# A token axis of 544 columns in halves of 272, where it had 546 in parts of 256 and 290

## The chip, the core and the metric

The kernel runs on one core of a Trainium2 chip. Its engines are named as the profile names them: PE is TensorE's matrix unit and PEld its weight loads, DVE is VectorE, ACT is ScalarE, POOL is GpSimd and SP is SyncE. The metric is the device time of one execution in microseconds (us), and a kernel's time is the median of its runs. The TensorE clock that was granted over the profiled execution of the kernel before is 0.999 of full speed, which is the upper one of its two levels, 2.4 GHz.

## The reference

One inference step of a two-layer encoder for two request groups: a prompt of 512 tokens and a sample of 32 tokens with caches. Everything is fp32. Cut to what the change touches:

```python
def conv_ffn(h, hist, w_up, conv_w, conv_b, w_down):
    S = h.shape[1]
    g, up = jnp.split(h @ w_up, 2, axis=-1)
    gp = jnp.concatenate([hist, g], axis=1)
    c = conv_b + sum(conv_w[j] * gp[:, j:j + S] for j in range(CONV_W))
    a = jax.nn.silu(c) * up
    return a @ w_down, gp[:, -(CONV_W - 1):]

def trunk_layer(x, pos, past_k, past_v, mem_k, mem_v, conv_hist, w, lam_init):
    h = rmsnorm(x, w['norm_mix_g'])
    z = h @ w['w_in']
    ...
    x = x + jnp.concatenate([o, g_out], axis=-1) @ w['w_out']
    x = x + cross_attend(rmsnorm(x, w['norm_x_g']), mem_k, mem_v, ...)
    f, conv_state = conv_ffn(rmsnorm(x, w['norm_ffn_g']), conv_hist, ...)
    return x + f, k, v, gv, conv_state
```

The model has 1024 features and 2816 hidden features of the FFN (22 tiles of 128). The convolution runs over three tokens: a token's own gate row and the two before it. The prompt starts with two rows of zeros, the sample with the two rows of `state_ffn_conv`.

## The kernel before

**The token axis.** Most of the network is computed with features on the 128 partitions and tokens along the free axis. Prompt and sample lie side by side on one axis of T = 546 columns: 512 prompt tokens, 2 columns of padding (set to zero in most tiles), and 32 sample tokens from column S0 = 514. The two padding columns serve the convolution: the tile of gate rows `gb` has two zero columns, then the 546 token columns, and the sample's two history rows are copied into the padding, so that one shifted pass over the whole tile computes the convolution of both groups.

**Exact products.** A weight tile is loaded raw by DMA (SP's queue), then split by ACT (L133) and DVE (L134) into a high and a low part, `hl[:, 0]` and `hl[:, 1]`; activations are split likewise. `hx` (the residual, [128, 8, 2, T]), `at` (the FFN's hidden rows, [128, 2, T]), `og` and `gg` (mixer outputs) and `co` (cross-attention outputs) hold the high part in `[.., 0, :]` and the low part in `[.., 1, :]`, in fp32r, 4 bytes an element. So the low part of a row starts T x 4 = 2184 bytes behind the high part.

**The projections.** `proj_fm` (its matmul is L263) makes one output tile of 128 features for all tokens. For each k tile it makes three passes: weights high x activations high, weights high x activations low, weights low x activations high. Each pass is a pair of matmuls, one for each part of the token axis in NSPL, into two PSUM banks whose tiles end in "a" (256 columns) and "b" (290 columns). The stationary operand is a 128 x 128 block of weights and the moving operand is a part of an activation row:

```python
for hl, ks, first, last in parts:
    for j, (kk, rh, rl) in enumerate(ks):
        for wpart, mv, st in ((0, rh, True), (0, rl, False), (1, rh, False)):
            for n0, nn in NSPL:
                pe.matmul(out=ps[0 if n0 == 0 else 1][:, 0:nn], ...
                          rhs=mv[:, n0:n0 + nn], ...)
```

A projection of 8 k tiles is 24 pairs (`pfg` and `pfu` of the FFN's gate and up rows, `pq`, `pu`, `pwo`, `pwc`); a down projection of the FFN (`pfd`) has 11 k tiles in each half of the hidden features, 33 pairs. Other projections (`tm_group`, L280 to L282, tiles `pr` and `pm`) have tokens on partitions: their stationary operand is an activation block, and their moving operand is the weight tile itself, 256 columns, first `hl[:, 0]`, then `hl[:, 1]`, then `hl[:, 0]`. The cross-attention's output (L875, `pxo`) moves the whole 512 columns of a tile `pT` of the prompt alone.

**The FFN.** For a hidden tile f: the gate projection into `pfga` and `pfgb`; DVE scales both into `gb` (L910); POOL clears two columns (L908), copies the sample's history into `gb` (L911) and keeps the last rows in `fc` (L912, L913); ACT makes the convolution's first term (L914); DVE adds the other two (L917); ACT and DVE finish SiLU (L919, L920); and the up projection, multiplied in, is split into `at`. PSUM has three pairs of banks for these projections.

**The order of the work.** Each engine runs its own queue in order. A tile framework schedules the instructions of each engine by a simulated timeline of its own, so that the order in a queue isn't quite that of the source, and it adds the semaphore waits. Pools with a fixed number of buffers (5 of the tag that `gb`, `ct`, `th` and `up` share) make a writer wait until a buffer's last reader is done.

Of the kernel before, what the change touches and what calls it, by code (L numbers as in the profile page):

```python
# [13 lines left out]
ALU = mybir.AluOpType  # L14
# [4 lines left out]
SP = 512  # L19
# [6 lines left out]
T = 546          # tokens on the free axis: 512 prompt, 2 of padding, 32 sample  # L26
S0 = 514         # first sample token
NSPL = ((0, 256), (256, 290))
# [5 lines left out]
def encoder_step(ctx: ExitStack, tc: tile.TileContext, a, o):  # L34
# [31 lines left out]
    f32 = lambda ap: ap.bitcast(F32)  # L66
    MP = (slice(0, 64), slice(64, 128))

# [85 lines left out]
    def rsq(v, p, n, name, eng=vec):  # L154
        """1/sqrt of a compact tile: bit-level first guess, three Newton steps."""
        y, h, t = (tp.tile([128, n], F32, tag=f"{name}_{v}", bufs=2 if v == "y" else 1, name=name + v)
                   for v in "yht")
        yy, hh, tt = y[0:p, 0:n], h[0:p, 0:n], t[0:p, 0:n]
        eng.tensor_scalar(out=yy.bitcast(I32), in0=v.bitcast(I32), scalar1=-0.5, scalar2=1597463007.0,
                          op0=ALU.mult, op1=ALU.add)  # L160
        eng.tensor_scalar(out=hh, in0=v, scalar1=-0.5, scalar2=None, op0=ALU.mult)
        for _ in range(3):
            eng.tensor_tensor(out=tt, in0=yy, in1=yy, op=ALU.mult)
            eng.tensor_tensor(out=tt, in0=tt, in1=hh, op=ALU.mult)
            if eng is vec:
                vec.scalar_tensor_tensor(out=yy, in0=tt, scalar=1.5, in1=yy, op0=ALU.add, op1=ALU.mult)
            else:
                eng.tensor_scalar(out=tt, in0=tt, scalar1=1.5, scalar2=None, op0=ALU.add)
                eng.tensor_tensor(out=yy, in0=tt, in1=yy, op=ALU.mult)
        return y  # L170
# [5 lines left out]
    def gelu2(z, t):  # L176
        """z <- 2 * gelu(z), tanh form"""
        act.activation(out=t, in_=z, func=AF.Square, scale=math.sqrt(0.044715))
        vec.scalar_tensor_tensor(out=t, in0=t, scalar=1.0, in1=z, op0=ALU.add, op1=ALU.mult)
        act.activation(out=t, in_=t, func=AF.Tanh, scale=GC)  # L180
        vec.scalar_tensor_tensor(out=z, in0=t, scalar=1.0, in1=z, op0=ALU.add, op1=ALU.mult)

# [1 line left out]
    ssq_t = {}  # L184

    def set_hx(kt, g):
        """the gained residual as hi + lo"""
        xv = x[:, kt]
        act.activation(out=hx[:, kt, 0], in_=xv, func=AF.Copy, scale=g[:, kt:kt + 1])
        vec.scalar_tensor_tensor(out=hx[:, kt, 1], in0=xv, scalar=g[:, kt:kt + 1], in1=f32(hx[:, kt, 0]),  # L190
                                 op0=ALU.mult, op1=ALU.subtract)

    def set_sq(kt):
        """the sum of the residual's squares"""
        sq = tmp([128, T], "sqx")
        act.activation(out=sq, in_=x[:, kt], func=AF.Square)
        if kt == 0:
            ssq_t["x"] = G("t4", [128, T], "ssq")
            pool.tensor_copy(ssq_t["x"], sq)
        else:  # L200
            pool.tensor_tensor(out=ssq_t["x"], in0=ssq_t["x"], in1=sq, op=ALU.add)
# [16 lines left out]
    def x_stats(need_bc):  # L218
        """per token: v = mean square + eps, eps * v and 1/sqrt(v)"""
# [25 lines left out]
        pool.memset(rbc[:, SP:S0], 0.0)  # L245
        for i in range(2):
            pb = psS("pbc")
            for t in range(2):
                pe.matmul(out=pb[:, 128 * t:128 * t + 128], lhsT=ones, rhs=dg[:, 2 * i + t], start=True, stop=True)
            if i == 1:  # L250
                pe.matmul(out=pb[:, 256:288], lhsT=ones[0:32], rhs=dgs, start=True, stop=True)
                act.copy(rbc[:, S0:T], pb[:, 256:288])
            act.copy(rbc[:, 256 * i:256 * i + 256], pb[:, 0:256])  # L253
        return r, ve, rbc

# [1 line left out]
    def proj_fm(ps, col, parts):  # L257
        """features on partitions; parts: (weights [128, 2, n, 256], [(k in unit, rhs hi, rhs lo)], first, last)"""
# [111 lines left out]
    def load_consts2(l):  # L370
        """wider per-layer constants"""
# [11 lines left out]
    def norm_rope(z, p, nt, ss, rs, c, t0):  # L383
        """z [p, nt, 256] in place: QK-norm with 1/rms rs [p, nt * 4], gains, rotary"""
# [43 lines left out]
    def kq_T(l, h, z, zs):  # L428
        # of map m the rows MP[m] carry k's hi part, the others its lo part; q's hi part stands on both
# [45 lines left out]
    def softmax_diff(ps, p, n, e, c, name):  # L475
        """e[:, 0] <- exp(S0 - max) - lam * (sum0 / sum1) * exp(S1 - max); returns the sums"""
# [14 lines left out]
    def take_o(po, p, ot, ss):  # L491
        """head output rows out of PSUM, and their squares' sum"""
        junk = tmp([128, 128], "junk", tag="oh", bufs=1)
        act.copy(ot, po)
        act.activation(out=junk[0:p], in_=po, func=AF.Square, accum_out=ss)

    def subnorm(ot, sso, s0, p, n, name):
        """ot [p, n, 128]: head outputs; sso: their squares' sums; s0: softmax sums, where not yet divided by"""
# [77 lines left out]
    def do_attn_sample_end(l, hp, og, st):  # L576
        """the sample's head outputs of a pair of heads: norm, transpose"""
# [59 lines left out]
    def do_gate(l, j, vn, zs, ws):  # L637
        """the spatial gates of a pair of groups"""
        c = LC[l]
        res = []  # L640
        for jj in range(2):
# [10 lines left out]
            pool.memset(s[:, SP:S0], 0.0)  # L652
# [11 lines left out]
    def do_u(j, w2, rbc):  # L664
        """u of one group, times 2"""
        ps = psR2("pu")
        proj_fm(ps, j, x_parts(w2))
        u = tmp([128, T], "u")
        t1 = tmp([128, T], "ut")
        for v, n0, nn in halves(ps):  # L670
            vec.tensor_tensor(out=u[:, n0:n0 + nn], in0=v, in1=rbc[:, n0:n0 + nn], op=ALU.mult)
        gelu2(u, t1)
        return u
# [51 lines left out]
    def do_mem_k(l, h, mt, vm):  # L725
# [25 lines left out]
        # cached memory keys of the sample  # L751
# [23 lines left out]
    def do_cross_q(l, h, ve):  # L775
# [4 lines left out]
        for dc in range(2):  # L780
# [8 lines left out]
            act.copy(qs[:, dc], ps[1][:, S0 - 256:T - 256])  # L789
# [21 lines left out]
    def do_cross_scores(h, mk, cmT, qq):  # L811
# [36 lines left out]
        # sample tokens  # L848
# [42 lines left out]
    def do_ffn(l, rbc, after):  # L891
# [3 lines left out]
        for hf in range(2):  # L895
            av = []
            for f0 in range(hf * HF, hf * HF + HF, 2):
# [3 lines left out]
                for f in fs:  # L901
# [9 lines left out]
                    pool.tensor_copy(gb[:, SP + 2:SP + 4], c["st"][:, :, f])  # L911
# [4 lines left out]
                    for jj in (1, 0):  # L916
                        vec.scalar_tensor_tensor(out=ct, in0=gb[:, jj:jj + T], scalar=c["cw"][:, jj, f:f + 1],  # L917
                                                 in1=ct, op0=ALU.mult, op1=ALU.add)
                    act.activation(out=th, in_=ct, func=AF.Tanh, scale=0.5)  # L919
# [60 lines left out]
    for kt in range(8):  # L980
# [4 lines left out]
        vec.memset(ps[1][:, 256:258], 0.0)  # L985
        pe.transpose(ps[1][:, 258:290], xs[:, 128 * kt:128 * kt + 128], ident[0:32, 0:32])
        for i, (v, n0, nn) in enumerate(halves(ps)):
            (vec.tensor_copy if i else act.copy)(x[:, kt, n0:n0 + nn], v)
# [9 lines left out]
    for l in range(DEPTH):  # L998
# [5 lines left out]
        for t in og:  # L1004
            pool.memset(f32(t[:, :, SP:S0]), 0.0)
# [46 lines left out]
        for h in range(4):  # L1052
# [7 lines left out]
            for dc in range(2):  # L1060
                t = G(COTAGS[2 * h + dc], [128, 2, T], "co", F32R)
                pool.memset(f32(t[:, :, SP:S0]), 0.0)
# [27 lines left out]
def _rope_table():  # L1090
    """cos and signed sin of the rotary angles by position: a constant of the shapes alone"""
# [31 lines left out]
```

## Time and profile before

| | |
|---|---|
| time, median of 3 runs | 1721.8 us (1720.87 to 1721.93) |
| the profiled execution's own span | 1721.5 us |
| PE busy | 1700.7 us, 99% of the span, 13115 matmuls |
| PEld busy | 1641.7 us, 95% |
| DVE busy | 996.2 us, 58% |
| ACT busy | 728.9 us, 42% |
| POOL busy | 220.3 us, 13% |
| DMA | 158.03 MB, mean 92 GB/s |

The page gives one execution; the span runs from the first to the last instruction and is the only time of its own that the execution has, 0.3 us under the median. A matmul's duration in the profile overlaps that of the next one, since matmuls are pipelined; the time from one start to the next is what a matmul takes of the span. Both are read below.

### The profile page before, as it was taken

To read this page: it belongs to the slowest core of one execution; us is meant where nothing else is said; L and a number is where in the kernel's file an instruction comes from. 1 tells how busy PE (TensorE), PEld (TensorE's weight loads), DVE (VectorE), ACT (ScalarE), POOL (GpSimd) and SP (SyncE) were. 2 spreads that over 40 slices of the span, in tenths; PEclk is the share of its full clock that TensorE was granted. 3 is DMA by queue.
4 is the path that set the end of the run, shared out by engine and by line. 5 is a ranking of instruction groups with operands and counts; after the bars stand their busy time and mean duration, and the time that the engine had idled before them with its cause. 6 is when DMAs were issued, how large, how long until landed. Compare 5 with 4: busy or idle time off the path is not lost.

```text
span 1721.5 us, 32408 instructions
## 1 busy us (share of the span) xinstructions
PE 1700.7 (99%) x13115; PEld 1641.7 (95%) x13115; DVE 996.2 (58%) x2138; ACT 728.9 (42%) x1485; POOL 220.3 (13%) x624
## 2 busy tenths in 40 slices
PE   7999999999999999999999999999999999999998
PEld 6988899999999999999998888999999999999998
DVE  6778765565466624655367677655555665255642
ACT  5456754455333312333345576445543332133321
POOL 4000014221200000000111000422221000000000
PEclk9999999999999999999999999999999999999999
DMA  5222233442222233223332222243422322333131
GB/s 174 89 86 71 66 102 100 141 130 82 86 79 88 70 88 108 86 68 87 93 117 70 76 69 85 85 130 105 129 81 74 99 62 86 101 94 90 55 115 57
DMA packets 200988, 158.03 MB, mean 92 GB/s; under 512 B 8670, under 2 KB 200038, under 8 KB 200838
## 3 DMA queue, kind: packets, MB, share of 16 engines
q1 hardware_dynamic: 200774, 155.82, 29.8%
q8 instruction: 103, 1.69, 0.4%
q14 instruction: 47, 0.39, 0.1%
q10 hardware_dynamic: 64, 0.14, 0.0%
HBM read 144.83 MB, written 11.10 MB: 91 GB/s over the span
## 4 chain that ended last, share of the span: by engine, by line
PE 95%; ACT 1%; POOL 1%; DVE 1%; issue 1%; SPq 1%; DMA 0%; ACTq 0%; DVEq 0%
PE pfgb L263 8%; PE pfub L263 8%; PE pfdb L263 8%; PE pfua L263 7%; PE pfga L263 7%; PE pfda L263 7%; PE pr L282 4%; PE pr L280 4%; PE pr L281 4%; PE pwob L263 3%; PE pqb L263 3%; PE pwcb L263 3%; PE pwoa L263 3%; PE pwca L263 3%; PE pqa L263 3%; PE pub L263 2%
## 5 line engine op out<-in xcount | busy, mean ns | idle before, releaser
L134 DVE TENSOR_TENSOR hl<-raw,hl 128x1024 fp32r<-128x1024 f32 (+2 forms) x280 | 317.1, 1133 | 278.0 <-ACT hl L133 277.6
L133 ACT CAST hl<-raw 128x1024 fp32r<-128x1024 f32 (+2 forms) x280 | 269.9, 964 | 408.8 <-PE pfdb L263 139.2
L263 PE MATMUL pfgb<-hx,hl 128*128 128x290 f32 x1056 | 269.6, 297 | 0.0
L263 PE MATMUL pfdb<-at,hl 128*128 128x290 f32 x1056 | 269.5, 298 | 0.0
L263 PE MATMUL pfga<-hx,hl 128*128 128x256 f32 x1056 | 269.3, 283 | 0.0
L263 PE MATMUL pfda<-at,hl 128*128 128x256 f32 x1056 | 268.4, 282 | 0.0
L263 PE MATMUL pfub<-hx,hl 128*128 128x290 f32 x1056 | 264.9, 297 | 0.0
L263 PE MATMUL pfua<-hx,hl 128*128 128x256 f32 x1056 | 264.2, 283 | 0.5 <-ACT rbc L253 0.5
L263 PEld LDWEIGHTS pfdb<-at,hl 128*128 128x128 f32 x1056 | 200.4, 190 | 0.1
L263 PEld LDWEIGHTS pfgb<-hx,hl 128*128 128x128 f32 x1056 | 200.4, 190 | 0.0
L263 PEld LDWEIGHTS pfda<-at,hl 128*128 128x128 f32 x1056 | 200.0, 189 | 0.0
L263 PEld LDWEIGHTS pfga<-hx,hl 128*128 128x128 f32 x1056 | 199.6, 189 | 0.0
L263 PEld LDWEIGHTS pfub<-hx,hl 128*128 128x128 f32 x1056 | 198.3, 190 | 0.0
L263 PEld LDWEIGHTS pfua<-hx,hl 128*128 128x128 f32 x1056 | 196.9, 189 | 0.7 <-ACT rbc L253 0.7
L282 PE MATMUL pr<-hl,hx 128*128 128x256 f32 x512 | 147.8, 290 | 2.4 <-DVE hx L190 2.4
L280 PE MATMUL pr<-hl,hx 128*128 128x256 f32 x512 | 147.5, 289 | 1.4 <-DVE vs L305 0.9
L281 PE MATMUL pr<-hl,hx 128*128 128x256 f32 x512 | 147.6, 289 | 0.8 <-DVE hl L134 0.8
L282 PEld LDWEIGHTS pr<-hl,hx 128*128 128x128 f32 x512 | 98.0, 192 | 5.8 <-DVE hx L190 2.8
L281 PEld LDWEIGHTS pr<-hl,hx 128*128 128x128 f32 x512 | 98.3, 192 | 3.6 <-issue 1.7
L280 PEld LDWEIGHTS pr<-hl,hx 128*128 128x128 f32 x512 | 98.0, 192 | 3.7 <-DVE vs L305 1.1
L263 PE MATMUL pwcb<-co,hl 128*128 128x290 f32 x384 | 88.7, 298 | 0.0
L917 DVE SCALAR_TENSOR_TENSOR ct<-gb,cols,ct 128x546 f32<-128x546 f32 x88 | 69.3, 787 | 33.2 <-ACT ct L914 31.6
(360 smaller groups left out, 3312.7 us busy)
## 6 DMA issues: line engine op xcount, KB each, us to landing
raw<-in_w_up_dram SPq DMA_DIRECT2D x80, 512.0 KB
raw<-in_w_down_dram SPq DMA_DIRECT2D x32, 512.0 KB
raw<-in_w_in_dram SPq DMA_DIRECT2D x24, 512.0 KB
raw<-in_w_in_dram SPq DMA_DIRECT2D x32, 256.0 KB
raw<-in_w_out_dram SPq DMA_DIRECT2D x32, 256.0 KB
raw<-in_wq_c_dram SPq DMA_DIRECT2D x16, 512.0 KB
raw<-in_wk_c_dram SPq DMA_DIRECT2D x16, 512.0 KB
raw<-in_wv_c_dram SPq DMA_DIRECT2D x16, 512.0 KB
```

The costliest lines, as they stand in the source:

```text
L133: act.copy(hl[:, 0, 0:n * wc], raw[:, 0:n * wc])
L134: vec.tensor_tensor(out=hl[:, 1, 0:n * wc], in0=raw[:, 0:n * wc], in1=f32(hl[:, 0, 0:n * wc]), op=ALU.subtract)
L263: pe.matmul(out=ps[0 if n0 == 0 else 1][:, 0:nn], lhsT=hl[:, wpart, kk, col * 128:col * 128 + 128], rhs=mv[:, n0:n0 + nn], start=first and ...
L280: pe.matmul(out=out, lhsT=lh(k), rhs=hl[:, 0, k % 4], start=(k == 0), stop=False)
L281: pe.matmul(out=out, lhsT=lh(k), rhs=hl[:, 1, k % 4], start=False, stop=False)
L282: pe.matmul(out=out, lhsT=ll(k), rhs=hl[:, 0, k % 4], start=False, stop=(k == k8 - 1))
L917: vec.scalar_tensor_tensor(out=ct, in0=gb[:, jj:jj + T], scalar=c["cw"][:, jj, f:f + 1], in1=ct, op0=ALU.mult, op1=ALU.add)
```

## The change

The two padding columns go: T is 544, the sample starts at column 512, and the two parts of the axis are equal halves of 272. The memsets of the padding go with it (in `rbc`, `s`, `og`, `co` and the input's PSUM tile), and the two copies of `rbc`'s second part become one. The convolution can no longer find the sample's history in `gb`. It runs over all 544 columns as before, which leaves the first two sample columns of `ct` wrong, and these two are computed apart: `gs` is a tile of four columns (two of history, two of the sample's first gate rows), `ge` one of two columns; three more POOL instructions and two more DVE instructions for each of the 44 hidden tiles (22 in each layer) take the place of one POOL copy.

```diff
-T = 546          # tokens on the free axis: 512 prompt, 2 of padding, 32 sample
-S0 = 514         # first sample token
-NSPL = ((0, 256), (256, 290))
+T = 544
+S0 = 512
+TH = T // 2
+NSPL = ((0, TH), (TH, TH))
...
-        pool.memset(rbc[:, SP:S0], 0.0)
...
-                act.copy(rbc[:, S0:T], pb[:, 256:288])
-            act.copy(rbc[:, 256 * i:256 * i + 256], pb[:, 0:256])
+            act.copy(rbc[:, 256 * i:256 * i + 256 + 32 * i], pb[:, 0:256 + 32 * i])
...
-            pool.memset(s[:, SP:S0], 0.0)
...
-            act.copy(qs[:, dc], ps[1][:, S0 - 256:T - 256])
+            act.copy(qs[:, dc], ps[1][:, S0 - TH:T - TH])
...
-                    pool.tensor_copy(gb[:, SP + 2:SP + 4], c["st"][:, :, f])
+                    gs = tiny([128, 4], "gs")
+                    ge = tiny([128, 2], "ge")
+                    pool.tensor_copy(gs[:, 0:2], c["st"][:, :, f])
+                    pool.tensor_copy(gs[:, 2:4], gb[:, S0 + 2:S0 + 4])
+                    pool.tensor_scalar(out=ge, in0=gs[:, 2:4], scalar1=c["cw"][:, 2, f:f + 1],
+                                       scalar2=c["cb"][:, f:f + 1], op0=ALU.mult, op1=ALU.add)
                     pool.tensor_copy(fc[:, 0:2, f], gb[:, SP:SP + 2])
                     pool.tensor_copy(fc[:, 2:4, f], gb[:, T:T + 2])
                     act.activation(out=ct, in_=gb[:, 2:T + 2], func=AF.Identity, scale=c["cw"][:, 2, f:f + 1],
...
                     for jj in (1, 0):
                         vec.scalar_tensor_tensor(out=ct, in0=gb[:, jj:jj + T], scalar=c["cw"][:, jj, f:f + 1],
                                                  in1=ct, op0=ALU.mult, op1=ALU.add)
+                    vec.scalar_tensor_tensor(out=ge, in0=gs[:, 1:3], scalar=c["cw"][:, 1, f:f + 1], in1=ge,
+                                             op0=ALU.mult, op1=ALU.add)
+                    vec.scalar_tensor_tensor(out=ct[:, S0:S0 + 2], in0=gs[:, 0:2], scalar=c["cw"][:, 0, f:f + 1],
+                                             in1=ge, op0=ALU.mult, op1=ALU.add)
...
-        vec.memset(ps[1][:, 256:258], 0.0)
-        pe.transpose(ps[1][:, 258:290], xs[:, 128 * kt:128 * kt + 128], ident[0:32, 0:32])
-        for i, (v, n0, nn) in enumerate(halves(ps)):
-            (vec.tensor_copy if i else act.copy)(x[:, kt, n0:n0 + nn], v)
+        pe.transpose(ps[1][:, 256:288], xs[:, 128 * kt:128 * kt + 128], ident[0:32, 0:32])
+        act.copy(x[:, kt, 0:256], ps[0][:, 0:256])
+        vec.tensor_copy(x[:, kt, 256:T], ps[1][:, 0:288])
...
-        for t in og:
-            pool.memset(f32(t[:, :, SP:S0]), 0.0)
...
-                pool.memset(f32(t[:, :, SP:S0]), 0.0)
```

The change makes each activation row 544 x 4 = 2176 bytes long, which is 34 x 64; 546 x 4 = 2184 bytes was 34 x 64 + 8. The second half starts at byte 1088 = 17 x 64 of its row, where it started at byte 1024 = 16 x 64. The tiles that L263 moves start at multiples of 32 bytes, `hx` at a multiple of 64, before and after; so with 2176 every part starts at a multiple of 32, and with 2184 every low part of a row starts 8 bytes off a multiple of 16.

DVE's queue in the FFN, from a gate projection's scaling to the end of SiLU (first layer; `hl` rows belong to the weight stream). Before:

```order
L910 TENSOR_TENSOR gb<-pfga,rbc 128x256
L910 TENSOR_TENSOR gb<-pfgb,rbc 128x290
L917 SCALAR_TENSOR_TENSOR ct<-gb,cols_253,ct 128x546 x2
L134 TENSOR_TENSOR hl<-raw,hl 128x512
L920 SCALAR_TENSOR_TENSOR ct<-th,ct 128x546
```

The same place now (`cols` holds the convolution's weights):

```order
L908 TENSOR_TENSOR gb<-pfga,rbc 128x272
L908 TENSOR_TENSOR gb<-pfgb,rbc 128x272
L923 SCALAR_TENSOR_TENSOR ge<-gs,cols_245,ge 128x2
L921 SCALAR_TENSOR_TENSOR ct<-gb,cols_245,ct 128x544 x2
L925 SCALAR_TENSOR_TENSOR ct<-gs,cols_245,ge 128x2
L135 TENSOR_TENSOR hl<-raw,hl 128x512
L928 SCALAR_TENSOR_TENSOR ct<-th,ct 128x544
```

The scheduler has put the first small step, which reads `ge` from POOL, right behind the scaling and ahead of the two long steps, which wait for ACT.

POOL's queue between two gate projections of the same stretch (`st` is the sample's history). Before:

```order
L908 MEMSET gb 128x2
L911 COPY gb<-st_259 128x2
L912 COPY fc<-gb 128x2
L913 COPY fc<-gb 128x2
L908 MEMSET gb 128x2
```

The same place now:

```order
L906 MEMSET gb 128x2
L913 COPY gs<-gb 128x2
L916 COPY fc<-gb 128x2
L917 COPY fc<-gb 128x2
L914 TENSOR_SCALAR ge<-gs,cols_245 128x2
L912 COPY gs<-st_251 128x2
L906 MEMSET gb 128x2
```

The history's copy no longer stands between the scaling and ACT's first term: it goes into `gs`, ahead of the next projection. The step that DVE waits for, L914, stands fourth behind the scaling.

## Rows read from the trace of the kernel before

**Rows 1.** Busy time of engines, from the page.

```profile
PE 1700.7 (99%) x13115; PEld 1641.7 (95%) x13115; DVE 996.2 (58%) x2138; ACT 728.9 (42%) x1485; POOL 220.3 (13%) x624
```

**Rows 2.** PE's waits: for what, total us, times, longest.

```profile
PE pxina L983 <- DMA xin<-in_x_prompt_dram: 5.3, 1, 5.3
...
PE pfua L263 <- ACT rbc L253: 0.5, 2, 0.2
```

**Rows 3.** L263 by group: count | busy us, mean ns | idle before.

```profile
L263 PE MATMUL pfgb<-hx,hl 128*128 128x290 f32 x1056 | 269.6, 297 | 0.0
...
L263 PE MATMUL pwcb<-co,hl 128*128 128x290 f32 x384 | 88.7, 298 | 0.0
...
L263 PE MATMUL pub<-hx,hl 128*128 128x290 f32 x192 | 39.3, 307 | 0.0
```

**Rows 4.** 100 us of FFN: busy us and count of PE, PEld, DVE, ACT, POOL; clock.

```profile
700.00:800.00 100.00, 100.00 (x788) 100.00 (x788) 61.89 (x93) 34.43 (x44) 4.72 (x31) 1.00 0.26 78
```

**Rows 5.** PE's timeline in down projections: start us, duration us, line, tiles.

```profile
600.29 0.30 PE L263 MATMUL pfub<-hx,hl 128*128 128x290 f32 x1
600.43 0.29 PE L263 MATMUL pfda<-at,hl 128*128 128x256 f32 x1
...
608.80 0.28 PE L263 MATMUL pfda<-at,hl 128*128 128x256 f32 x1
...
609.04 0.29 PE L263 MATMUL pfda<-at,hl 128*128 128x256 f32 x1
...
609.30 0.28 PE L263 MATMUL pfda<-at,hl 128*128 128x256 f32 x1
...
609.55 0.28 PE L263 MATMUL pfda<-at,hl 128*128 128x256 f32 x1
...
609.81 0.29 PE L263 MATMUL pfda<-at,hl 128*128 128x256 f32 x1
...
610.07 0.28 PE L263 MATMUL pfda<-at,hl 128*128 128x256 f32 x1
...
610.32 0.28 PE L263 MATMUL pfda<-at,hl 128*128 128x256 f32 x1
...
610.57 0.28 PE L263 MATMUL pfda<-at,hl 128*128 128x256 f32 x1
...
610.83 0.28 PE L263 MATMUL pfda<-at,hl 128*128 128x256 f32 x1
...
611.08 0.28 PE L263 MATMUL pfda<-at,hl 128*128 128x256 f32 x1
```

**Rows 6.** PE's timeline in a stream of 256-column matmuls with weights moving.

```profile
292.58 0.28 PE L281 MATMUL pm<-hl,memT 128*128 128x256 f32 x1
292.69 0.28 PE L282 MATMUL pm<-hl,memT 128*128 128x256 f32 x1
...
303.81 0.29 PE L282 MATMUL pm<-hl,memT 128*128 128x256 f32 x1
```

**Rows 7.** PE's timeline around six matmuls of 512 columns.

```profile
358.94 1.57 PE L875 MATMUL pxo<-pT,mvs 128*128 128x512 f32 x6
360.35 0.84 PE L263 MATMUL pqb<-hx,hl 128*128 128x290 f32 x5
```

**Rows 8.** Timeline of DVE, POOL and ACT behind one gate projection.

```profile
704.30 0.45 DVE L910 TENSOR_TENSOR gb<-pfgb,rbc 128x290 f32<-128x290 f32 x1
704.81 0.19 POOL L911 COPY gb<-st 128x2 f32<-128x2 f32 x1 [5.64 <-DVE gb L910]
...
705.05 0.84 ACT L914 ACTIVATE ct<-gb,cols 128x546 f32<-128x546 f32 x1
705.18 1.23 DVE L134 TENSOR_TENSOR hl<-raw,hl 128x1024 fp32r<-128x1024 f32 x1 [0.43 <-ACT hl L133]
706.32 0.78 DVE L917 SCALAR_TENSOR_TENSOR ct<-gb,cols,ct 128x546 f32<-128x546 f32 x1
```

**Rows 9.** Small instructions by group: count | busy us, mean ns | idle before.

```profile
L733 DVE SCALAR_TENSOR_TENSOR mss<-mss,vm 128x2 f32<-128x2 f32 x8 | 1.2, 148 | 0.0
L168 POOL TENSOR_SCALAR rmkt<-rmkt 128x2 f32<-128x2 f32 x24 | 5.4, 223 | 2.1
L985 DVE MEMSET pxinb<- 128x2 f32 x8 | 0.5, 60 | 2.0 <-PE pxinb L983 2.0
L1062 POOL MEMSET co<- 128x4 f32 x16 | 1.6, 103 | 51.8 <-PE pg L646 30.2 <-PE pmt L709 17.7 <-PE pwob L263 3.9
```

## The prediction

> **What bounds the kernel now.** I begin with the page's busy times. PE is busy for 1700.7 of 1721.5 us, so it stands still for 20.8 us; DVE works for 58% and POOL for 13% [rows 1]. Since overlapped matmuls can look busy without being at their peak, I then ask for PE's waits. The longest is the first load of the input, 5.3 us; of the terms that the change touches, PE waits 0.5 us in all for the copies of `rbc` [rows 2]. So no stall is worth removing here, and the time is the number of matmuls times what each takes from start to start.
>
> Most of them are those of `proj_fm`. Its second-half matmuls count 1056 each in `pfg`, `pfu` and `pfd` (the row of one stands), 384 each in `pwc` and `pq`, 192 each in `pu` and the two kinds of `pwo`, with no idle time before them worth a term [rows 3]: 3 x 1056 + 2 x 384 + 3 x 192 = 4512 pairs. The durations there (297 to 307 ns) are not the price, for they overlap. The price is in the stretch from 700 to 800 us, which is FFN alone: 788 matmuls in 100 us at a granted clock of 1.00 [rows 4], 126.9 ns each, 253.8 ns a pair of 256 and 290 columns. All pairs together are 4512 x 253.8 ns = 1145 us, two thirds of the span.
>
> **What the change does to a pair.** It takes 2 of 546 columns away, evens out the halves, and moves the start of every second row. I price these from streams.
>
> First the columns. The tokens-on-partitions products move weights in blocks of 256 columns, from tiles whose parts all start at multiples of 32 bytes: 95 starts after 292.58 us the stream is at 303.81 [rows 6], 118.2 ns each. Six matmuls of 512 columns, also from such a tile, take from 358.94 to 360.35 [rows 7], 235 ns each. Between the two lengths a column costs (235 - 118.2) / 256 = 0.456 ns. Two columns less are 0.91 ns a pair, 4512 x 0.91 = 4.1 us in all.
>
> Then the halves. On that line 256 and 290 columns would take 118.2 + 133.7 = 251.9 ns, and twice 272 takes 2 x (118.2 + 16 x 0.456) = 251.0. A straight line doesn't care how 544 is shared out, so evening out by itself is worth nothing. But the pairs take 253.8 and not 251.9: something costs 1.9 ns more than the line.
>
> What that is, the down projections show. They begin at 600.43, where `pfd` follows `pfu`; one is 33 pairs, so the next begins 33 x 0.2538 = 8.37 us later, at 608.80 [rows 5]. From there the starts of the first half follow the code's three passes (high, low, low weights). Over three k tiles the first passes take 0.24, 0.26, 0.25, the second 0.26, 0.26, 0.26, the third 0.25, 0.25, 0.25 us: 0.250 a pair where the high part of `at` is moved, 0.260 where the low part is. The low part is what starts 2184 bytes further on, 8 bytes off every multiple of 16. That the values are low, or that the second pass has the weights of the first, isn't it by the other stream: there L281 moves the low part of a tile as well, against the stationary block of L280, and the low part starts 4096 bytes behind the high one; its step to the next start is 0.11 us, no longer than the mean of 0.118 [rows 6]. So I put the extra time down to where the row starts. From what multiple on a start is a good one, these rows can't say; 2176 keeps all of those that the high parts have.
>
> With the change the low parts start as the high ones do. For a pair afterwards I have two values. By the line it is 251.0. By the high passes in the down projections it is 250.0 less two columns, 249.1. The second comes from one tile group with starts read to 10 ns; the first rests on long streams, though of other operands. I take 250.6, nearer to the line. The saving is 3.2 ns a pair, 4512 x 3.2 = **14.4 us**. The ends are 253.8 - 249.1 = 4.7 ns, or 21.2 us, and the two columns alone, 4.1 us.
>
> The Trainium skill, "TensorE: Matmul & The Clock Gate", section "Back-to-back issue gap", gives an isolated warm matmul N / 2.4 + 2.5 ns, with no term for an operand's address. An estimate from it is 232.5 ns for a pair before and 231.7 after, 3.8 us in all over these pairs; the trace disagrees with its level (253.8) and agrees roughly with its slope (0.456 against 0.417 ns a column). By that rule only the columns would count, which is the first rival below.
>
> **What it does elsewhere.** Eight DVE memsets of 60 ns go from the input, and POOL memsets of about 0.1 us each from `co`, `og`, `s` and `rbc` [rows 9]. PE waits for none of them for more than the 0.5 us of `rbc` [rows 2], so I count nothing; the uncovered price of all is some 4 us of POOL time (36 memsets of 103 ns) and 0.5 of DVE's.
>
> The convolution loses one POOL copy (0.19 us [rows 8]) and gains three POOL instructions and two on DVE for each of 44 hidden tiles. The nearest rows for these are 0.15 us for a 128 x 2 step on DVE and 0.22 for one on POOL [rows 9]; so DVE has 0.3 us more to do in each, 13 us in all, and POOL about 0.4. Where they lie matters more. DVE's first small step now stands right behind the scaling and waits for POOL's fourth instruction. The scaling ended at 704.75, POOL's copy started at 704.81 and ACT's first term at 705.05 [rows 8]; four POOL steps of about 0.2 us put `ge` at some 705.6. What is queued behind that step is the weight split of DVE, which in this place started at 705.18, and the long steps, which ran from 706.32. The split could thus start 0.4 us later. ACT's first term no longer waits for POOL's copy and may start 0.2 us sooner. Who waits for all that is PE, through PSUM banks and weights; but a gate projection takes 24 x 0.254 = 6.1 us, there are three pairs of banks, and DVE works for 62% of this stretch [rows 4]. I take 0. If that cover were gone, 44 x (0.3 + 0.4) = 31 us would be the price.
>
> The sum: 1721.5 - 14.4 = 1707.1 us for the execution profiled, whose span is 0.3 under the median of the runs; so 1707.4 us as a median.
>
> **The rivals.** A change of 0.2% (3.4 us) is about what a measurement of this kernel can tell from none.
>
> *Only the columns count.* Then the slow second pass has another cause and stays: 253.8 - 0.91 = 252.9 a pair, 1721.8 - 4.1 = 1717.7 us. For it speaks that the rows show starts to 10 ns only, and that the line's streams read other tiles. Against it, the second pass is the longer in each of three k tiles. Chance 0.14; since 4.1 us is just over the bound, 0.09 of it counts as faster.
>
> *Another set of addresses is as bad.* If what costs time isn't the odd start but moving and weight reads that fall on each other, a new set of addresses may do no better: pairs at 253.8 again, 1722 us. Against it: the stream of 256 columns has both operands at such starts and is the fast one [rows 6]. Chance 0.07, 0.02 of it slower (were all pairs as the slow 0.260, less 0.9 ns, it would be 4512 x 5.3 ns = 24 us, 1746).
>
> *DVE's queue holds up PE (slower).* The place is the small step that waits for POOL, with the weight split behind it. To outweigh 14.4 us, each of the 44 hidden tiles would have to hold PE up by more than 0.33 us; with the 0.7 of above unhidden it is 1721.8 - 14.4 + 31 = 1738 us. For it: the split is what PE's next weights come from. Against it: DVE is free for 38% of that stretch, and PE had no wait for it there. Chance 0.05.
>
> **How the numbers follow.** My forecast has 0.74. It is faster; with 0.09 of the first rival that makes 0.83. Within 0.2%: 0.05 of the first and 0.05 of the second, 0.10. Slower: 0.02 and 0.05, 0.07. The predicted time is that of the likeliest, 1707.4. The range goes from the high passes' value (21.2 us saved, 1700.6) to the columns alone (1717.7): 1700.5 to 1718; outside stay the last two rivals, 0.12, and what the forecast may miss by.
>
> **What would show it.** Right: an FFN stretch of 100 us holds about 798 matmuls (100 / 0.1253) where it held 788; in a down projection the three passes take the same time, about 0.250; PE's waits stay near 20 us; and the 256-column stream stays at 118 ns, since nothing of it changes. The first rival shows as 791 matmuls and a second pass still at 0.259. The third shows as PE idle before `pfg` and `pfu`, put down to DVE's `hl` or `gb`. The forecast is wrong if the starts aren't what made the second pass slow, or if 272 columns are off the line between 256 and 512, which no row here shows.

## The result, and the profile after

The changed kernel takes 1703.8 us (median of 4 runs, 1703.65 to 1704.66) against 1721.9 us of the kernel before in the same job: 18.1 us less, a ratio of 0.9895 with a 95% interval of 0.9881 to 0.9910. That lies in the predicted range, below the predicted 1707.4. The profiled execution has a span of 1702.9 us.

The busy times of the engines after, from the page, beside [rows 1]:

```profile
PE 1683.1 (99%) x13115; PEld 1623.8 (95%) x13115; DVE 1006.2 (59%) x2218; ACT 727.5 (43%) x1481; POOL 250.4 (15%) x676
```

PE makes as many matmuls as before and stands still for 19.8 us (20.8 before). So the gain isn't a stall that went; the matmuls follow each other faster. Its waits, beside [rows 2]; the same two are there, the first 0.5 us longer:

```profile
PE pxina L991 <- DMA xin<-in_x_prompt_dram: 5.8, 1, 5.8
...
PE pfua L262 <- ACT rbc L252: 0.5, 2, 0.2
```

The 100 us of FFN beside [rows 4] hold 805 matmuls where they held 788:

```profile
700.00:800.00 100.00, 100.00 (x805) 100.00 (x805) 63.56 (x109) 33.65 (x43) 10.00 (x43) 1.00 0.28 81
```

PE's timeline in the down projections, beside [rows 5]; the second one begins 33 pairs behind 594.34, at 602.62 (start us, duration us):

```profile
594.34 0.29 PE L262 MATMUL pfda<-at,hl 128*128 128x272 f32 x1
...
602.62 0.29 PE L262 MATMUL pfda<-at,hl 128*128 128x272 f32 x1
...
602.87 0.29 PE L262 MATMUL pfda<-at,hl 128*128 128x272 f32 x1
...
603.12 0.29 PE L262 MATMUL pfda<-at,hl 128*128 128x272 f32 x1
...
603.38 0.29 PE L262 MATMUL pfda<-at,hl 128*128 128x272 f32 x1
...
603.62 0.29 PE L262 MATMUL pfda<-at,hl 128*128 128x272 f32 x1
...
603.88 0.29 PE L262 MATMUL pfda<-at,hl 128*128 128x272 f32 x1
...
604.13 0.29 PE L262 MATMUL pfda<-at,hl 128*128 128x272 f32 x1
...
604.38 0.29 PE L262 MATMUL pfda<-at,hl 128*128 128x272 f32 x1
...
604.63 0.29 PE L262 MATMUL pfda<-at,hl 128*128 128x272 f32 x1
...
604.88 0.29 PE L262 MATMUL pfda<-at,hl 128*128 128x272 f32 x1
```

The three passes now take 0.74, 0.76 and 0.76 us over three k tiles, where they took 0.75, 0.78 and 0.75: the second is no longer the long one. (602.62 - 594.34) / 33 is 0.251 us a pair.

The convolution's stretch beside [rows 8], the timeline of DVE, POOL and ACT behind one gate projection:

```profile
690.93 0.43 DVE L908 TENSOR_TENSOR gb<-pfgb,rbc 128x272 f32<-128x272 f32 x1
691.39 0.84 ACT L918 ACTIVATE ct<-gb,cols 128x544 f32<-128x544 f32 x1 [4.57 <-DVE gb L908]
691.42 0.18 POOL L913 COPY gs<-gb 128x2 f32<-128x2 f32 x1 [12.38 <-DVE gb L908]
...
691.82 0.35 POOL L914 TENSOR_SCALAR ge<-gs,cols 128x2 f32<-128x2 f32 x1
692.21 0.22 DVE L923 SCALAR_TENSOR_TENSOR ge<-gs,cols,ge 128x2 f32<-128x2 f32 x1 [0.85 <-POOL ge L914]
692.34 1.60 DVE L921 SCALAR_TENSOR_TENSOR ct<-gb,cols,ct 128x544 f32<-128x544 f32 x2
```

ACT starts 0.03 us behind the scaling, where it started 0.30 behind it. DVE does stand still for `ge`; over all 44 tiles the wait is this row (total, times, longest):

```profile
DVE ge L923 <- POOL ge L914: 26.5, 44, 0.9
```

DVE needs 10 us more than before and waits 26.5 us at a new place. That PE's time doesn't change by it is shown below, by a version without the small tile.

### The profile page after: what moved, and what is told of

It reads as the page before. It is cut to its first block, busy times and chain, and to the rows that moved or that the text cites. A ratio compares the mean times of both kernels' runs of the same rounds, so it can differ in the third digit from the quotient of the medians.

```text
span 1702.9 us, 32510 instructions
## 1 busy us (share of the span) xinstructions
PE 1683.1 (99%) x13115; PEld 1623.8 (95%) x13115; DVE 1006.2 (59%) x2218; ACT 727.5 (43%) x1481; POOL 250.4 (15%) x676
## 4 chain that ended last, share of the span: by engine, by line
PE 95%; ACT 1%; DVE 1%; SPq 1%; POOL 1%; DMA 0%; issue 0%; ACTq 0%
PE pfda L262 8%; PE pfua L262 8%; PE pfga L262 8%; PE pfdb L262 8%; PE pfub L262 8%; PE pfgb L262 8%; PE pr L281 4%; PE pr L279 4%; PE pr L280 4%; PE pwob L262 3%; PE pwoa L262 3%; PE pwca L262 3%; PE pqb L262 3%; PE pqa L262 3%; PE pwcb L262 3%; PE pm L281 2%
## 5 line engine op out<-in xcount | busy, mean ns | idle before, releaser
L262 PE MATMUL pfda<-at,hl 128*128 128x272 f32 x1056 | 266.6, 289 | 0.0
L262 PE MATMUL pfdb<-at,hl 128*128 128x272 f32 x1056 | 266.3, 288 | 0.0
L262 PE MATMUL pfga<-hx,hl 128*128 128x272 f32 x1056 | 263.8, 287 | 0.0
L262 PE MATMUL pfgb<-hx,hl 128*128 128x272 f32 x1056 | 263.7, 287 | 0.0
L262 PE MATMUL pfua<-hx,hl 128*128 128x272 f32 x1056 | 259.3, 287 | 0.5 <-ACT rbc L252 0.5
L262 PE MATMUL pfub<-hx,hl 128*128 128x272 f32 x1056 | 259.1, 287 | 0.0
L262 PE MATMUL pwcb<-co,hl 128*128 128x272 f32 x384 | 87.1, 288 | 0.0
L262 PE MATMUL pwca<-co,hl 128*128 128x272 f32 x384 | 86.9, 289 | 0.0
## 6 DMA issues: line engine op xcount, KB each, us to landing
raw<-in_w_in_dram SPq DMA_DIRECT2D x32, 256.0 KB
raw<-in_w_out_dram SPq DMA_DIRECT2D x32, 256.0 KB
```

The source lines that it names most:

```text
L262: pe.matmul(out=ps[0 if n0 == 0 else 1][:, 0:nn], lhsT=hl[:, wpart, kk, col * 128:col * 128 + 128], rhs=mv[:, n0:n0 + nn], start=first and ...
```

## The experiments

All ratios are to the kernel before, in the same job (a batch of runs on one chip). Its median was 1721.6 to 1723.3 us in the different jobs, so between jobs a difference under 2 us is not read. To see where in the kernel a version gains, I count matmuls in two stretches that hold nothing else than pairs: 675 to 785 us (gate and up projections, which move `hx`) and 602 to 658 us (down projections, which move `at`). Of the kernel before and of the changed one the two rows are:

```profile
675.00:785.00 110.00, 110.00 (x867) 110.00 (x866) 68.81 (x101) 37.01 (x47) 4.99 (x36) 1.00 0.26 77
602.00:658.00 56.00, 56.00 (x444) 56.00 (x444) 15.59 (x27) 11.08 (x14) 0.00 (x0) 1.00 0.33 94
```

```profile
675.00:785.00 110.00, 110.00 (x886) 110.00 (x886) 71.43 (x121) 36.78 (x46) 12.13 (x51) 1.00 0.27 80
602.00:658.00 56.00, 56.00 (x449) 56.00 (x448) 17.18 (x28) 10.42 (x13) 0.00 (x0) 1.00 0.35 103
```

A count takes in the matmuls that overlap an edge, so 220 us or 112 us over it comes out about 0.5 to 2 ns too low for a pair, and one matmul more or less is 0.3 ns for `hx` and 0.6 for `at`. The pair times below are therefore means over the trace, from the start of one pair to the start of the next, for the 80 gate and up projections (1920 pairs) and the 24 down projections (792 pairs) whose pairs follow each other without a break; the counts stand in brackets. By the same reading the 253.8 ns that the prediction took from [rows 4] is 254.4.

| kernel | us | ratio (95%) | pair of `hx`, ns | pair of `at`, ns |
|---|---|---|---|---|
| before | 1721.9 | 1 | 254.4 (867) | 253.6 (444) |
| changed | 1703.8 | 0.9895 (0.9881 to 0.9910) | 248.9 (886) | 251.2 (449) |
| rows 2184 again | 1710.7 | 0.9933 (0.9919 to 0.9948) | 252.0 (875) | 251.8 (447) |
| before, rows of `hx` 2240 | 1719.2 | 0.9983 (0.9974 to 0.9992) | 253.3 (871) | 253.5 (444) |
| all tiles at 64 | 1705.3 | 0.9902 (0.9887 to 0.9916) | 251.1 (879) | 251.2 (448) |
| `hx` at 32, rest at 64 | 1709.9 | 0.9928 (0.9912 to 0.9945) | 251.1 (878) | 251.2 (448) |
| parts 256 and 288 | 1708.6 | 0.9916 (0.9902 to 0.9931) | 252.2 (874) | 249.0 (452) |
| both undone | 1713.0 | 0.9943 (0.9928 to 0.9957) | 252.7 (873) | 251.4 (448) |
| no small tile | 1704.2 | 0.9891 (0.9875 to 0.9908) | 248.9 (886) | 251.2 (448) |
| `at` and others 96 further on | 1703.4 | 0.9886 (0.9871 to 0.9901) | 248.9 (886) | 251.2 (448) |
| before, 288 of 290 | 1714.8 | 0.9956 (0.9942 to 0.9970) | 252.8 (873) | 251.9 (448) |
| before, 286 of 290 | 1711.9 | 0.9937 (0.9924 to 0.9949) | 251.9 (876) | 251.1 (448) |
| 256 of each 272 | 1657.0 | 0.9619 (0.9606 to 0.9632) | 238.6 (925) | 238.1 |
| halves for `hx`, 256 and 288 for the rest | 1701.4 | 0.9875 (0.9862 to 0.9889) | 248.9 (887) | 249.0 (452) |

**Rows 2184 bytes apart again.** My theory was that of the prediction: where a row starts is worth most. The rival: only columns and halves count.

```diff
+TS = T + 2
...
-    hx = cp.tile([128, 8, 2, T], F32R, name="hx")
+    hx = cp.tile([128, 8, 2, TS], F32R, name="hx")[:, :, :, 0:T]
...
-        og = [G("og", [128, 2, T], "og", F32R) for _ in range(4)]
+        og = [G("og", [128, 2, TS], "og", F32R)[:, :, 0:T] for _ in range(4)]
```

(and so for `gg`, `co`, `xq` and `at`)

> The changed kernel with the rows of hx, at, og, gg and co stored 546 columns apart again (2184 bytes), 544 of them used, halves of 272 as in the change. Theory (what the change gains is mostly where rows start): low parts start 8 bytes off again, so the second pass of each k tile is the longer one again, by 5 to 7 ns a pair; a pair takes about 253 ns where it now takes about 250, and 4512 pairs give back 13 to 15 us: 1717 to 1719 us. Rival (only the number of columns and the equal halves count): nothing of the gain is lost, 1704 us, with three equal passes.

6.9 us are lost, half of what was expected. It is nearly all in the pairs of `hx`, which go from 248.9 to 252.0 ns; those of `at` lose 0.6. For `at` the slow second pass does not come back. PE's timeline of this kernel from the start of its second down projection:

```profile
603.57 0.29 PE L263 MATMUL pfda<-at,hl 128*128 128x272 f32 x1
...
603.82 0.29 PE L263 MATMUL pfda<-at,hl 128*128 128x272 f32 x1
...
604.08 0.29 PE L263 MATMUL pfda<-at,hl 128*128 128x272 f32 x1
...
604.33 0.29 PE L263 MATMUL pfda<-at,hl 128*128 128x272 f32 x1
...
604.57 0.28 PE L263 MATMUL pfda<-at,hl 128*128 128x272 f32 x1
...
604.82 0.28 PE L263 MATMUL pfda<-at,hl 128*128 128x272 f32 x1
...
605.07 0.29 PE L263 MATMUL pfda<-at,hl 128*128 128x272 f32 x1
```

The second passes take 0.26 and 0.25 us, the first 0.25 and 0.24, the third 0.25 and 0.25, with the low parts 8 bytes off as in [rows 5]. So for `at` the odd start alone isn't what made them long. For `hx` the second pass does come back as the longest: over the same projections as in the table the three passes take 251.5, 254.1 and 250.3 ns here, 246.7, 250.0 and 250.0 in the changed kernel and 254.2, 256.8 and 252.3 in the kernel before. But the first pass, whose start is a multiple of 16 in either, loses more (4.8 ns) than the second (4.1).

**The kernel before with rows of `hx` 2240 bytes apart.**

```diff
-    hx = cp.tile([128, 8, 2, T], F32R, name="hx")
+    hx = cp.tile([128, 8, 2, 560], F32R, name="hx")[:, :, :, 0:T]
...
-        skq = tmp([128, 352], "skq", tag="skq", bufs=2)
+        skq = tmp([128, 352], "skq", tag="skq", bufs=1)
```

> The kernel before, 546 columns in 256 and 290, its padding and its convolution as they were, but the rows of hx stored 560 columns apart (2240 bytes, 35 x 64); to make room the tile skq has one buffer instead of two. Theory: the 2688 pairs that move hx lose their slow second pass and go from 254 to about 250 ns (249 of the changed kernel and 0.9 for two columns), 11 us: 1711 us; an FFN stretch of gate and up projections holds 800 matmuls in 100 us where it held 788, and down projections keep their slow second pass. Rival (columns and halves): 1722 us, 788 matmuls. If the one buffer costs a wait it shows on PE before the sample's attention, below 2 us.

Good starts alone, at 546 columns in 256 and 290, gain 0.17%, 3 us of the 11 expected: pairs of `hx` go from 254.4 to 253.3 and not to 250. PE's timeline of this kernel from the start of an up projection:

```profile
701.45 0.29 PE L263 MATMUL pfua<-hx,hl 128*128 128x256 f32 x1
...
701.71 0.28 PE L263 MATMUL pfua<-hx,hl 128*128 128x256 f32 x1
...
701.96 0.29 PE L263 MATMUL pfua<-hx,hl 128*128 128x256 f32 x1
...
702.22 0.28 PE L263 MATMUL pfua<-hx,hl 128*128 128x256 f32 x1
...
702.47 0.28 PE L263 MATMUL pfua<-hx,hl 128*128 128x256 f32 x1
...
702.72 0.28 PE L263 MATMUL pfua<-hx,hl 128*128 128x256 f32 x1
...
702.97 0.29 PE L263 MATMUL pfua<-hx,hl 128*128 128x256 f32 x1
...
703.23 0.28 PE L263 MATMUL pfua<-hx,hl 128*128 128x256 f32 x1
...
703.48 0.29 PE L263 MATMUL pfua<-hx,hl 128*128 128x256 f32 x1
...
703.74 0.28 PE L263 MATMUL pfua<-hx,hl 128*128 128x256 f32 x1
```

The second pass, 0.75 us over three k tiles, is now the shortest, and the first and third take 0.77. As means over the trace the passes go from 254.2, 256.8 and 252.3 ns to 256.0, 249.4 and 254.5: the second one gains 7.4 ns, as the theory has it, and the two whose rows were thought good lose 4.0 together. Both theories miss, the first because it counted on those two to stay.

**Which start is good?** Two versions move whole tiles and leave row lengths and halves as in the change. In the changed kernel `hx` starts at a multiple of 64, weights and the other tiles 32 bytes behind one.

```diff
     xsm = cp.tile([128, 8, 64], F32R, name="xsm")
+    pad = cp.tile([128, 8], F32, name="pad")
+    vec.memset(pad, 0.0)
```

> The changed kernel with 32 bytes of filling behind xsm, so that weights and every activation tile start at a multiple of 64, where in the changed kernel hx starts at one and the weights and at, og, gg and co start 32 bytes behind one. Theory A (a moved row is fastest from a multiple of 64): pairs that move at, og, gg and co go from 251 to 249 ns as those of hx are, 1824 x 2.1 = 3.8 us, and the 2560 matmuls of 256 columns that move weights from about 119 to 118, some 2 us: 1698 us. Theory B (moving and weight reads are slower when both start alike within 64 bytes): the pairs of at stay at 251 and those of hx go from 249 to 251, 2688 x 2.1 = 5.6 us: 1709 us. If multiples of 16 or 32 are all alike: 1704 us and all pairs as they were.

```diff
+    pad = cp.tile([128, 8], F32, name="pad")
...
     hx = cp.tile([128, 8, 2, T], F32R, name="hx")
+    pad2 = cp.tile([128, 8], F32, name="pad2")
...
     xsm = cp.tile([128, 8, 64], F32R, name="xsm")
+    pad3 = cp.tile([128, 8], F32, name="pad3")
...
```

> The changed kernel with hx 32 bytes behind a multiple of 64 and the weights and all other activation tiles at one: the starts of hx and of the rest change places. Theory A (a moved row is fastest from a multiple of 64): pairs of hx go from 249 to 251 ns, pairs of at, og, gg and co from 251 to 249, and weights moved as 256 columns from 119 to 118; in time 5.6 - 3.8 - 2 = 0, about 1704 us; 100 us of gate and up projections hold 797 matmuls, not 805. Theory B (both operands starting alike is what is slow): pairs of hx stay at 249, those of at stay at 251 (both start alike still), 1704 us and 805 matmuls.

In the first, `hx` keeps its address, and its pairs go from 248.9 to 251.1 ns because the other tiles moved by 32 bytes; `at`, now at 64, isn't faster. Theory A falls. Its time, 1705.3, is not to be told from the changed kernel's, because another stream gains most of what the pairs lose (4.1 us): the products with tokens on partitions that move weights against blocks of `hx` (`pr`, 1536 matmuls) go from 118.5 to 116.4 ns each, 3.2 us in all. In the second, `hx` and the weights start differently within 64 bytes, and the pairs of `hx` still take 251.1. Theory B falls too. What the two show is that a pair's time doesn't hang on the moving row's start alone. Whether it hangs on where the two operands lie to each other or on the weights' own start they don't tell, since the weights start at a multiple of 64 in both.

**Equal halves, and halves and rows together.**

```diff
-NSPL = ((0, TH), (TH, TH))
+NSPL = ((0, 256), (256, 288))
...
-            act.copy(qs[:, dc], ps[1][:, S0 - TH:T - TH])
+            act.copy(qs[:, dc], ps[1][:, S0 - 256:T - 256])
```

> The changed kernel with the 544 columns in parts of 256 and 288, all else as it is (rows 2176 bytes apart). Theory 1 (only where a row starts counts, a part's length by a straight line): 1704 us, a pair of hx at 249 ns and one of at at 251. Theory 2 (equal halves are worth something by themselves, as the kernel with rows of hx 560 columns apart and parts of 256 and 290 hints, 253.2 ns a pair): 252.3 ns a pair for all, (252.3 - 249.0) x 2688 + (252.3 - 251.1) x 1824 = 11 us more, 1715 us.

The next version, with both undone, has this diff and that of the rows 2184 bytes apart.

> The changed kernel with both undone: rows 2184 bytes apart and parts of 256 and 288; 544 columns, no padding and the small tile of the convolution remain. What is left against the kernel before is the two columns, the convolution and the memsets: by 0.46 ns a column 1721.7 - 4 = 1718 us, a slow second pass as before. If equal halves and row starts work only together, this and the kernel with parts of 256 and 288 alone should be alike; if they add, it is 7 us above that.

With both undone 1713.0 us; good rows alone 1708.6, halves alone 1710.7, both 1703.8. They add 4.4 and 2.3, together 9.2. The 2.3 is between two jobs and the intervals of its two ratios overlap, so by the times alone it is not shown. For the pairs of `hx` it is starker: 252.7 with neither, 252.2 with good rows, 252.0 with halves, 248.9 with both. For `at` halves are no gain at all: 249.0 in 256 and 288, 251.2 in halves, both with good rows. Theory 1 (nothing from halves) and theory 2 (11 us more, all pairs at 252.3 ns) both miss.

**The small tile.**

```diff
-                    gs = tiny([128, 4], "gs")
-                    ge = tiny([128, 2], "ge")
...
-                    vec.scalar_tensor_tensor(out=ct[:, S0:S0 + 2], in0=gs[:, 0:2], scalar=c["cw"][:, 0, f:f + 1],
-                                             in1=ge, op0=ALU.mult, op1=ALU.add)
```

> The changed kernel without the small tile: gs, ge and their five instructions are left out, so the convolution of the sample's first two tokens reads the last prompt rows instead of the sample's history. Theory (hidden behind PE): 1704 us, within 1 us. Rival (DVE's wait for POOL holds up weights): up to 0.7 us for each of 44 hidden tiles, as low as 1673 us.

1704.2 us: it costs nothing that can be measured.

**A distance within 128 bytes?**

```diff
+    gpad = gp.tile([128, 24], F32, name="gpad")
+    vec.memset(gpad, 0.0)
     GB = {"og": 4, "kq": 4, "v": 3, "zr": 2, "e": 2, "p": 2, "t4": 2}
```

> The changed kernel with 96 bytes of filling ahead of at, og, gg and co, so that these stand to the weights' address, within 128 bytes, as hx does (moving start 96 bytes ahead of a weight block's, modulo 128, both halves taken together). In the changed kernel a pair of hx takes 249.0 ns and one of the others 251.1; when weights were moved by 32 bytes, pairs of hx went to 251.1. Theory (the distance between the moving row and the weights within 128 bytes decides these 2 ns): pairs of at, og, gg and co go to 249, 1824 x 2.1 = 3.8 us: 1700 us, the fastest version. Rival (something of hx's own rows does it, or a longer distance): 1704 us, pairs at 251.

1703.4 us, and pairs of `at` stay at 251.2 ns. This rule falls as well.

**The price of two columns.** In the kernel before, with every address as it is:

```diff
+                        n = nn if first and j == 0 and st or last and j == len(ks) - 1 and wpart == 1 else min(nn, 288)
-                        pe.matmul(out=ps[0 if n0 == 0 else 1][:, 0:nn],
+                        pe.matmul(out=ps[0 if n0 == 0 else 1][:, 0:n],
                                   lhsT=hl[:, wpart, kk, col * 128:col * 128 + 128],
-                                  rhs=mv[:, n0:n0 + nn],
+                                  rhs=mv[:, n0:n0 + n],
```

> The kernel before, addresses and all, but in 22 of the 24 passes of a projection (31 of 33 in a down projection) the second matmul moves 288 columns, not 290: the products of the sample's last two tokens are left out there. It is the price of two columns by itself, on 4160 of the 4512 pairs. Theory L (a straight line, 0.456 ns a column): 4160 x 0.91 = 3.8 us, 1718 us. Theory S (a part's length costs more when it is no multiple of some count of columns, as the 8.7 us between the kernel before and the one with 544 columns, rows 2184 bytes apart and parts of 256 and 288 hint): about 1.8 ns a pair, 7.6 us, 1714 us.

> The same with 286 columns, four of 290 left out. Theory L: 4160 x 1.82 = 7.6 us, 1714 us, twice what 288 gave. Theory S: 286 is no multiple either, so it takes as long as 288 or longer: 1714 us or above, no gain over 288.

The first two columns are worth 0.44%, 7.6 us (5 to 10), as theory S has it and twice the line. The next two bring it to 0.63%, 10.9 us (8.8 to 13.1): some 3 us more, which theory S denies. Pair by pair the first two are worth 1.6 ns with `hx` and 1.7 with `at`, the next two 0.9 and 0.8. The line gives 0.8 and 0.9 (0.91 x 22 / 24 and 0.91 x 31 / 33): it holds for the second two columns and is half of what the first two cost.

**Halves of 256.**

```diff
+                        n = nn if first and j == 0 and st or last and j == len(ks) - 1 and wpart == 1 else 256
```

> The changed kernel, but in the same 22 of 24 (31 of 33) passes both matmuls move only the first 256 columns of their half, so the products of 16 tokens in each half are left out there. It shows whether 272 columns stand on the line between 256 and 512: by 0.456 ns a column 4160 x 32 x 0.456 = 60.7 us less, 1643 us, by 1 / 2.4 ns a column 55.5 us less, 1648 us.

1657.0 us: 46.8 us less than the changed kernel, not 55 to 61. From 272 to 256 a column gives 46.8 / (4160 x 32) = 0.35 ns by the times. That is a little low, for PE now waits 3.6 us for ACT where it did not before (`pg` for `gz`); by the steps of all pairs, 52.8 us less, it is 0.40. The 272 columns of `hx` lie below the line between 256 and 512 (248.9 ns a pair where the line gives 251.0), those of `at` on it (251.2).

**The best parts for each operand.**

```diff
+XSPL = ((0, 256), (256, 288))
...
-                proj_fm(ps, i, o_parts(w2, co))
+                proj_fm(ps, i, o_parts(w2, co), XSPL)
```

(and so for `wout`, the down projections and `update_x`)

> The changed kernel with halves of 272 for the projections that move hx, and parts of 256 and 288 for those that move at, og, gg and co (wout, wo and down projections), addresses as they are. Pairs of hx took 249.0 ns in halves and 252.0 in 256 and 288, those of the others 251.1 and 249.0 at the same addresses. If each kind keeps its own price, 1824 x 2.1 = 3.8 us less than the changed kernel: 1700 us, all pairs at 249, the fastest version. If a pair's price hangs on what the neighbouring projections do, it is anything between 1700 and 1709.

Each kind keeps its price: 248.9 and 249.0 ns. The two rows of this version:

```profile
675.00:785.00 110.00, 110.00 (x887) 110.00 (x886) 71.14 (x121) 37.38 (x48) 11.87 (x51) 1.00 0.26 78
602.00:658.00 56.00, 56.00 (x452) 56.00 (x452) 16.04 (x27) 10.97 (x13) 0.00 (x0) 1.00 0.35 103
```

It is the fastest, 1701.4 us with a span of 1698.9; its interval just overlaps that of the changed kernel, so the 2.4 us between the two are shown by the pairs of `at` (452 matmuls in 56 us where there were 449) rather than by the times.

## Why the prediction was right, and where it was off

*PE's step from start to start is the time.* Right. PE stands still as long as before, and the pairs carry the gain: added up over the two traces (waits above 0.4 us left out), the steps of the 2688 pairs of `hx` are 13.8 us shorter, 5.1 ns a pair, and those of the 1824 others 4.9 us, 2.7 ns a pair. That is 18.7 us, against 18.6 between the two spans.

*The two columns: 4.1 us.* The term was mis-sized. Going from 290 to 288 by itself gave 7.6 us (5 to 10), in the passes of 4160 of the 4512 pairs. And the version with both undone, which has 544 columns, the new convolution and no padding, has nearly the pair times of the kernel before with 288 (252.7 and 252.8 ns for `hx`, 251.4 and 251.9 for `at`): little else on that way counts. The step that failed is the straight line through [rows 6] and [rows 7]: a slope over 256 columns gave half of what these two cost, though it fits the next two.

*Where rows start: 10.3 us.* Mis-sized, and its mechanism too simple. Undoing it costs 4.4 us at parts of 256 and 288 and 6.9 at halves. That the second pass is the longest where its row starts odd holds for `hx` in all parts tried (251.4, 254.7 and 251.9 ns in 256 and 288). The step that failed is the one behind "With the change the low parts start as the high ones do": that the second pass would then take what the others take, and these stay as they were. With good starts and 290 columns the second pass gains 7.4 ns and the other two lose 4.0 together, so a pair of `hx` gains 1.1 ns where some 4 were due. And for `at`, from which the prediction had read it, the second pass is as short as the others with the odd start and 272 columns: the long pass of [rows 5] needed the start and the length together.

*Evening out is worth nothing.* Failed for `hx` (3.3 ns a pair with good rows), and for `at` the other way round, which loses 2.2.

*A pair afterwards: 250.6, between 251.0 and 249.1.* Pairs of `hx` take 248.9, just below the lower end, those of `at` 251.2, just above the upper one. That the total came out near the forecast was in part luck: a term that was too small (the columns), one that was too large (the rows) and one that was left out (the halves) partly met.

*The convolution is hidden.* Right, and shown by leaving it out. Its pieces were underpriced (0.22 us a small step on DVE where 0.15 was taken, 0.35 for POOL's where 0.22 was), and DVE's wait is there, 26.5 us in all, but the time without the small tile is the same. That it is the three pairs of banks that cover the wait is argued, not shown.

*The 256-column stream stays at 118 ns, since nothing of it changes.* Wrong. Beside [rows 6], the changed kernel's stream:

```profile
290.15 0.28 PE L281 MATMUL pm<-hl,memT 128*128 128x256 f32 x1
...
301.42 0.28 PE L281 MATMUL pm<-hl,memT 128*128 128x256 f32 x1
```

94 starts later it is at 301.42: 119.9 ns each, not 118.2. I had overlooked that shorter rows move every tile that is allocated behind them; within 64 bytes the weights moved by 32. But the weights' start by itself is not the cause. Over the whole trace a step of this stream takes 118.1 ns before and 120.0 in the changed kernel; with rows 2184 bytes apart, where the weights start 32 bytes behind a multiple of 64 as well, it takes 118.0, and with all tiles at 64, where they are back at a multiple of 64, 119.8. With the weights as in the changed kernel and the pool that holds `memT`, the stationary operand, 96 bytes further on it takes 118.0 again.

*The rivals.* "Only the columns" is out: with 544 columns alone (both undone) 1713.0, not 1717.7, and the change lies 9.2 us below. "Another set of addresses is as bad" was wrong of this change, though the thing that it names, the two operands' addresses together, is among those that may be at work: moving the weights and the tiles behind them by 32 bytes cost the pairs of `hx` 2.2 ns. An estimate from the Trainium skill's formula in "TensorE: Matmul & The Clock Gate", section "Back-to-back issue gap", gives a pair 0.8 ns for two columns. The runs agree for the step from 288 to 286 (0.9 and 0.8) and not for that from 290 to 288 (1.6 and 1.7).

What stays open is the rule by which addresses and lengths set a matmul's step. Three simple ones were tried and fell: the moving row's start within 64 bytes, its start against the weights' within 64, and the same within 128. That it is reads of the two operands meeting in the memory is a guess that no run here tests. Starts 8 and 16 bytes off with all rows alike were not tried. Nor was a move of the weights alone.

## What to carry to other kernels

Where PE is busy all the time, price a change of shape by the step from start to start, and suspect every length and row pitch: 2 of 546 columns were worth 0.44%, and equal halves with even rows another 0.5%, though neither alone was. Such a gain belongs to one set of addresses: filling of 32 bytes moved pairs by 2 ns, curing one pass lengthened the other two, and the best parts were not the same for two operands of one kernel, so try a few pitches and splits on the chip and don't take a line through long streams for short steps. And look at what a shorter tile moves behind it.

## What the runs showed of the hardware that was not expected

At a granted clock of 1.00 and with nothing to wait for, a pair of matmuls over the same 544 columns took from 248.9 to 252.7 ns on average, by where the operands lay and how the columns were shared out. `hx` at an unchanged address became 2.2 ns a pair slower when the other tiles moved by 32 bytes. Streams of 256 columns with weights moving changed by addresses as well: against `memT` 120.0 ns a matmul in the changed kernel and 118.0 with `memT`'s pool 96 bytes further on, against `hx` 118.5 in the changed kernel and 116.4 with all tiles at 64. In the pairs two columns from 290 to 288 were worth 1.6 to 1.7 ns, and the next two 0.8 to 0.9.
